# Down projections of a two-layer trunk: 20 of 22 tiles in seven block products, two in plain passes between them, and second weight sums requested from the third product on

## The chip, the cores and the metric

The kernel runs on one core of a Trainium2 chip. The metric is the device time of one execution in microseconds (us). The engines' names are those of the profile: PE is TensorE (matmuls), PEld its weight loads, DVE VectorE, ACT ScalarE, POOL GpSimd, SP the engine that issues most transfers.

## The reference

Two layers; each is a half-step SwiGLU, a gated mixing of three attention branches, and another half-step SwiGLU, with an RMS norm before and after each part. There are 512 tokens of width 1024, the hidden width is 22 x 128 = 2816, and all data is fp32.

```python
def _swiglu(t, w_gate, w_up, w_down):
    return (jax.nn.silu(t @ w_gate) * (t @ w_up)) @ w_down
...
    for l in range(DEPTH):
        f = _swiglu(_rmsnorm(h, ffn1_pre_g[l]), ffn1_w_gate[l], ffn1_w_up[l], ffn1_w_down[l])
        h = h + 0.5 * _rmsnorm(f, ffn1_post_g[l])
        u = _rmsnorm(h, mix_pre_g[l])
        ...
        k_mem, v_mem = jnp.split(mem_n @ w_mem_kv[l], 2, axis=-1)
        ...
        h = h + _rmsnorm(merged @ w_out[l], mix_post_g[l])
        f = _swiglu(_rmsnorm(h, ffn2_pre_g[l]), ffn2_w_gate[l], ffn2_w_up[l], ffn2_w_down[l])
        h = h + 0.5 * _rmsnorm(f, ffn2_post_g[l])
```

What matters here is the last product of `_swiglu`, hidden (512 x 2816) by w_down (2816 x 1024), which occurs four times: the stages are called a0, c0 (the two SwiGLUs of the first layer) and a1, c1, and the mixing between them b0, b1. Also in play are the norm after it, the residual and the next norm, and the norm of the memory tokens, whose keys and values the mixing needs.

## The kernel before

**Arithmetic.** An fp32 matmul is done as three faster ones (`mm3`, L203 to L205) on a high and a low part of each operand. `split` makes the parts: ScalarE casts the high one (L189), VectorE subtracts it to get the low one (L190). So every block of weights of 256 rows by 512 columns (512 KB, in SBUF 128x1024) costs a transfer, a cast `wh_..` and a subtraction `wl_..`; four buffers of each (the tags wh and wl) and four landing tiles (raw) turn round.

**Block products.** A large matrix product is cut 2 x 2 by 2 x 2 and done in seven block products in place of eight, each of a sum of hidden blocks (`aa_..`, made by `first_factor` from the stored hidden halves `hra`) and a sum of weight blocks. `BlockUnit` is one such block of weights, of two 128-row tiles; its sums of two blocks are kept in `bta` tiles, made by a plain transfer followed by an accumulating one on POOL's queue (SUMS, products 2 and 5), or by VectorE's addition of a block onto a kept sum (products 3 and 6, L354). A product runs over both chunks (`ci`) of 8 k-tiles, and over two of the four tiles of 128 tokens (`e`). SUM gives the pair of PSUM banks in which a product accumulates, `pda_0_e`, `pda_1_e` or `pda_2_e`:

```python
    SUM = (0, 1, 2, 0, 2, 0, 0)
    TO = ((0, 0), (0, 0), (1, 1), (0, 1), (0, 1), (1, 1), (1, 0))
```

TO gives the token half and the column half into which the finished bank goes. Between uses by two outputs, a bank's content is copied or added into the result tile `fa_t` (t is the tile of 128 tokens), by ScalarE or by VectorE (L975); the next product then accumulates on top of what the bank holds.

**The down projection.** 16 of the 22 k-tiles go in seven products, in the order 0, 2, 3, 4, 5, 1, 6, and the other six plainly in `down` afterwards, one token tile's half after the other; banks are seeded there from `fa`, and `dst.result` takes the square (ScalarE) and the scaled result (VectorE).

**The order of the work.** A queue of jobs (class `Queue`) writes the program. A job's weights are loaded (cast and subtraction written out) before it starts, and so are those of the four next blocks (`load_ahead`, AHEAD = 4). When landing tiles come free, `fetch_ahead` issues transfers in the order of the jobs. A token tile's norm chain (`Sub.chain`: residual, square, norm, turning by four transposes per bank, split) is woven between matmuls, each step a given modelled time after the one before. Each engine then runs its instructions in the order written.

**Around the change.** The memory norm and the memory keys and values (`mem_norm`, `mem_kv`) come at the end of the first SwiGLU of each layer.

## Time and profile before

| | us |
|---|---|
| median of 3 runs (2341.53 to 2341.89) | 2341.72 |
| the profiled execution | 2341.6 |
| its span, first to last instruction | 2339.8 |
| TensorE busy (99%) | 2326.2 |
| VectorE busy (78%) | 1815.4 |
| ScalarE busy (61%) | 1429.4 |
| GpSimd busy (11%) | 246.6 |

The mean granted TensorE clock is 0.999. A timeline row gives start, duration, engine, line, operation, output and inputs, and in brackets how long the engine had been idle and what ended it. Rows of matmuls overlap: their spacing, not their duration, is what one costs. A row of the windows gives the window, its length, the busy time of each engine with the number of instructions, the clock, the DMA share and GB/s. The names in the profile leave the buffer numbers out, so `pda` is any bank of a0's or a1's down projection, `pdc` any of c0's or c1's.

### The profile page before, as it was taken

What the parts mean: (1) busy time and instruction counts of PE and PEld (TensorE: products, weight loads), DVE (VectorE), ACT (ScalarE), POOL (GpSimd) and SP (SyncE); (2) the same over time, 40 slices, a digit from 0 to 9 for tenths busy, and PEclk for the clock granted to TensorE, in tenths of its full rate; (3) what the DMA queues carried; (4) which work ended last, traced back from release to release, by engine and by line L of the source; (5) the groups of instructions that cost most, each with busy time, mean ns of one, the idle gap of its engine ahead of it and who ended that gap; (6) DMA issues with size and microseconds to landing.
All of it is one profiled execution on the core that took longest, in us unless ns stands there. A gap on an engine that the chain in (4) does not pass through costs nothing.

```text
span 2339.8 us, 32552 instructions
## 1 busy us (share of the span) xinstructions
PE 2326.2 (99%) x12232; PEld 1994.8 (85%) x12232; DVE 1815.4 (78%) x2407; ACT 1429.4 (61%) x2307; POOL 246.6 (11%) x330
## 2 busy tenths in 40 slices
PE   9999999999999999999999999999999999999998
PEld 8888889998888888888888888889988888888887
DVE  8766978676898887769887679786768988866696
ACT  6655766665665465567665567656656655556574
POOL 1101100100122011101011110011001210111110
PEclk9999999999999999999999999999999999999999
DMA  8866858753232676669586767587423326776682
GB/s 247 236 174 181 228 179 249 199 163 108 73 110 72 234 218 182 167 167 256 171 217 170 185 190 228 190 238 227 135 76 91 100 83 232 219 189 169 180 224 99
DMA packets 241697, 412.74 MB, mean 176 GB/s; under 512 B 12650, under 2 KB 78466, under 8 KB 241028
## 3 DMA queue, kind: packets, MB, share of 16 engines
q1 hardware_dynamic: 200992, 326.74, 42.5%
q0 software_dynamic: 37088, 71.34, 17.7%
q10 hardware_dynamic: 3460, 12.59, 1.4%
q8 instruction: 96, 1.57, 0.3%
q14 instruction: 61, 0.50, 0.1%
HBM read 383.35 MB, written 27.26 MB: 175 GB/s over the span
## 4 chain that ended last, share of the span: by engine, by line
PE 90%; DVE 5%; DMA 3%; ACT 1%; issue 1%; SPq 0%; POOL 0%; DVEq 0%; ACTq 0%; POOLq 0%
PE ptc L203 5%; PE ptc L205 5%; PE ptc L204 5%; PE pta L203 5%; PE pta L205 5%; PE pta L204 5%; PE g L203 3%; PE g L204 3%; PE g L205 3%; PE pdc L203 3%; PE pda L205 3%; PE pdc L205 3%; PE pdc L204 3%; PE pda L204 3%; PE pda L203 3%; PE pv L203 1%
## 5 line engine op out<-in xcount | busy, mean ns | idle before, releaser
L190 DVE TENSOR_TENSOR wl_tc<-ktc,wh_tc 128x1024 fp32r<-128x1024 f32 x80 | 97.7, 1223 | 63.3 <-ACT wh_tc L189 63.3
L190 DVE TENSOR_TENSOR wl_ta<-kta,wh_ta 128x1024 fp32r<-128x1024 f32 x80 | 97.6, 1223 | 57.8 <-ACT wh_ta L189 57.8
L205 PE MATMUL pta<-wh_ta,aga 128*128 128x512 f32 x320 | 124.7, 390 | 1.3 <-DVE aga L190 1.3
L189 ACT CAST wh_tc<-ktc 128x1024 fp32r<-128x1024 f32 x80 | 84.1, 1054 | 67.9 <-PE ptc L205 48.0
L203 PE MATMUL pta<-wh_ta,aga 128*128 128x512 f32 x320 | 125.2, 392 | 0.0
L203 PE MATMUL ptc<-wh_tc,agc 128*128 128x512 f32 x320 | 125.1, 393 | 0.0
L205 PE MATMUL ptc<-wh_tc,agc 128*128 128x512 f32 x320 | 124.6, 389 | 0.0
L204 PE MATMUL ptc<-wl_tc,agc 128*128 128x512 f32 x320 | 124.6, 389 | 0.0
L204 PE MATMUL pta<-wl_ta,aga 128*128 128x512 f32 x320 | 124.6, 389 | 0.0
L189 ACT CAST wh_ta<-kta 128x1024 fp32r<-128x1024 f32 x80 | 84.1, 1053 | 65.7 <-PE pta L205 41.8
L190 DVE TENSOR_TENSOR wl_tc<-raw_tc,wh_tc 128x1024 fp32r<-128x1024 f32 x56 | 68.6, 1224 | 45.4 <-ACT wh_tc L189 45.3
L190 DVE TENSOR_TENSOR wl_ta<-raw_ta,wh_ta 128x1024 fp32r<-128x1024 f32 x58 | 70.9, 1224 | 41.9 <-ACT wh_ta L189 41.8
L189 ACT CAST wh_ta<-raw_ta 128x1024 fp32r<-128x1024 f32 x58 | 60.9, 1052 | 45.5 <-PE pta L205 38.0
L189 ACT CAST wh_tc<-raw_tc 128x1024 fp32r<-128x1024 f32 x56 | 59.0, 1054 | 47.8 <-PE ptc L205 36.6
L203 PE MATMUL ptc<-wh_tc,us_b 128*128 128x512 f32 x224 | 87.7, 391 | 0.2
L203 PE MATMUL pda<-wh_da,aa 128*128 128x512 f32 x224 | 87.5, 391 | 0.0
L203 PE MATMUL pdc<-wh_dc,ac 128*128 128x512 f32 x224 | 87.5, 391 | 0.0
L205 PE MATMUL ptc<-wh_tc,us_b 128*128 128x512 f32 x224 | 87.2, 389 | 0.0
L204 PE MATMUL ptc<-wl_tc,us_b 128*128 128x512 f32 x224 | 87.2, 389 | 0.0
L205 PE MATMUL pda<-wh_da,aa 128*128 128x512 f32 x224 | 87.2, 389 | 0.0
L204 PE MATMUL pda<-wl_da,aa 128*128 128x512 f32 x224 | 87.2, 389 | 0.0
L204 PE MATMUL pdc<-wl_dc,ac 128*128 128x512 f32 x224 | 87.2, 389 | 0.0
(593 smaller groups left out, 7932.7 us busy)
## 6 DMA issues: line engine op xcount, KB each, us to landing
raw_ta<-in_ffn_w_gate_dram SPq DMA_DIRECT2D x44, 512.0 KB, 4.4
raw_tc<-in_ffn_w_gate_dram SPq DMA_DIRECT2D x44, 512.0 KB, 4.7
raw_da<-in_ffn_w_down_dram SPq DMA_DIRECT2D x42, 512.0 KB, 3.8
raw_dc<-in_ffn_w_down_dram SPq DMA_DIRECT2D x42, 512.0 KB, 3.6
kta<-in_ffn_w_up_dram SPq DMA_DIRECT2D x40, 512.0 KB, 6.2
raw_wg<-in_w_gate_dram SPq DMA_DIRECT2D x40, 512.0 KB, 4.7
ktc<-in_ffn_w_up_dram SPq DMA_DIRECT2D x40, 512.0 KB, 5.7
kt<-in_w_gate_dram SPq DMA_DIRECT2D x24, 512.0 KB, 5.9
```

The lines of the kernel that those rows point to most:

```text
L189: both = [nc.scalar.copy(h_ap, src)]
L190: make = lambda: nc.vector.tensor_tensor(l_ap, src, h_ap.bitcast(F32), ALU.subtract)
L203: nc.tensor.matmul(pt, lh, rh, start=start, stop=False, skip_group_check=free)
L204: nc.tensor.matmul(pt, lh, rl, start=False, stop=False, skip_group_check=free)
L205: nc.tensor.matmul(pt, ll, rh, start=False, stop=stop, skip_group_check=free)
```

## The change

Twenty of the 22 tiles go in seven products, in three chunks of 8, 8 and 4 k-tiles (ROWS = 4, 4, 2 rows of the 2 x 2 cut). Products 0, 2 and 1 are done for all chunks, then 3 and 4 interleaved, then 5 and 6 for all chunks. The two remaining tiles go in three plain passes, behind the products (2, 1), (1, 0) and (6, 0), written (product, chunk). Product 6's weights get block (1,0) by an accumulating transfer (`adds`) in place of VectorE's addition. The sums for product 5 are requested when the jobs (2, 0), (1, 0) and (3, 0) begin. Tokens 0 and 1 are finished when product 4 ends, tokens 2 and 3, one after the other, in the last chunk of product 6. `down` stays for the mixing's output alone. The memory tokens are normed and turned in a0's third group of gate products and saved to DRAM; they are loaded again at the job (6, 2), and their keys and values are made inside the mixing, behind its first three gate products. The steps of the norm chains are spaced by tables (W_A, W_C).

The largest of the moves, on TensorE, in a0. Before, where product 5 ends (banks `pda_0_..`) and the next product begins:

```order
L203 MATMUL pda_0_1_2101<-wh_da_1_5_2_2395,aa_0_5_2399 128x512
L204 MATMUL pda_0_1_2101<-wl_da_1_5_2_2396,aa_0_5_2399 128x512
L205 MATMUL pda_0_1_2101<-wh_da_1_5_2_2395,aa_0_5_2399 128x512
L203 MATMUL pda_1_0_2432<-wh_da_0_1_0_2436,aa_0_1_2482 128x512 [waits Activation_49]
L204 MATMUL pda_1_0_2432<-wl_da_0_1_0_2437,aa_0_1_2482 128x512 [waits DVE_49]
```

Now, at the same place; `wh_da_2_5_0` is the weight block of chunk 2, product 5, row 0:

```order
L203 MATMUL pda_0_1_2165<-wh_da_2_5_0_2781,aa_2_5_2849 128x512
L204 MATMUL pda_0_1_2165<-wl_da_2_5_0_2782,aa_2_5_2849 128x512
L205 MATMUL pda_0_1_2165<-wh_da_2_5_0_2781,aa_2_5_2849 128x512
L203 MATMUL pda_0_0_2164<-wh_da_0_6_0_2785,aa_0_6_2897 128x512 [waits DVE_49,Activation_49]
L204 MATMUL pda_0_0_2164<-wl_da_0_6_0_2786,aa_0_6_2897 128x512
```

Behind product 5 came product 1 in the banks `pda_1_..`; now comes product 6, in the banks that product 5 has just used. The wait on VectorE in its first row is for the addition of that bank into `fa_2`.

On VectorE, before, around that addition (L975):

```order
L354 TENSOR_TENSOR bta_1_0_1944<-bta_1_0_1944,raw_da_1_1_2_2318 128x1024 [waits DMAHW6_49]
L190 TENSOR_TENSOR wl_da_1_1_0_2475<-raw_da_1_1_0_2312,wh_da_1_1_0_2474 128x1024 [waits DVE_49,Activation_49]
L975 TENSOR_TENSOR fa_2_2094<-fa_2_2094,pda_0_0_2100 128x512 [waits PE_49]
L190 TENSOR_TENSOR wl_da_1_1_2_2479<-raw_da_1_1_2_2318,wh_da_1_1_2_2478 128x1024 [waits Activation_49]
L975 TENSOR_TENSOR fa_3_2095<-fa_3_2095,pda_0_1_2101 128x512 [waits PE_49]
```

Now (L1020), from the residual of token tile 1 on:

```order
L676 SCALAR_TENSOR_TENSOR ha_1_2753<-fa_1_2157,nfa_1_2744,ha_1_2753 128x1024 [waits DMAHW7_49,DVE_49]
L190 TENSOR_TENSOR wl_da_p_2844<-raw_da_p_2495,wh_da_p_2843 128x1024 [waits DMAHW6_49,Activation_49]
L581 TENSOR_SCALAR nha_0_2747<-nha_0_2747 128x1 [waits Activation_49]
L190 TENSOR_TENSOR wl_da_1_6_0_2890<-bta_1_0_2041,wh_da_1_6_0_2889 128x1024 [waits DMASW4_49,Activation_49]
L587 SCALAR_TENSOR_TENSOR nha_0_2747<-nha_0_2747 128x1 [waits DVE_49]
L581 TENSOR_SCALAR nha_1_2748<-nha_1_2748 128x1 [waits Activation_49]
L1020 TENSOR_TENSOR fa_2_2158<-fa_2_2158,pda_0_0_2164 128x512
L588 SCALAR_TENSOR_TENSOR nha_0_2747<-nha_0_2747 128x1 [waits DVE_49]
L587 SCALAR_TENSOR_TENSOR nha_1_2748<-nha_1_2748 128x1 [waits DVE_49,Activation_49]
L683 SCALAR_TENSOR_TENSOR fa_0_2156<-ha_0_2751,nha_0_2747,gqa_2799 128x1024 [waits DMAHW6_49,DVE_49]
L588 SCALAR_TENSOR_TENSOR nha_1_2748<-nha_1_2748 128x1 [waits DVE_49]
L1020 TENSOR_TENSOR fa_3_2159<-fa_3_2159,pda_0_1_2165 128x512 [waits PE_49]
```

The additions stood among the low parts of product 1's weights; now they stand behind the low part of the plain pass's block (`wl_da_p`), that of product 6's second chunk (`wl_da_1_6_0`), and the norm steps of tiles 0 and 1.

On TensorE at the very end (c1), the second half of tile 3 had a bank of its own (`pdc_0_3_1`; the first half's was `pdc_0_3_0`) and none of its rows had a wait. Now both halves are in the bank `pdc_0_1`; where the one ends and the other begins:

```order
L204 MATMUL pdc_0_1_20532<-wl_dc_2_6_0_21272,ac_2_6_21316 128x256
L205 MATMUL pdc_0_1_20532<-wh_dc_2_6_0_21271,ac_2_6_21316 128x256
L203 MATMUL pdc_0_1_20532<-wh_dc_2_6_0_21271,ac_2_6_21316 128x256 [waits DVE_49]
L204 MATMUL pdc_0_1_20532<-wl_dc_2_6_0_21272,ac_2_6_21316 128x256
L205 MATMUL pdc_0_1_20532<-wh_dc_2_6_0_21271,ac_2_6_21316 128x256
```

The row with the wait is the first of the second half; it is for the scaled result of the first half (L656).

The diff, cut to its core:

```diff
-        BLOCKS = {0: (0, 0), 3: (1, 1), 1: (1, 0), 6: (1, 0)}
+        BLOCKS = {0: (0, 0), 3: (1, 1), 4: (1, 1), 1: (1, 0), 6: (1, 0)}
         SUMS = {2: (0, (0, 1), (0, 0)), 5: (1, (1, 1), (0, 1))}
...
-            return self.n in self.BLOCKS and self.twin is None
+            return self.n in self.BLOCKS and self.twin is None and not self.adds
...
+            if self.adds:
+                self.block(self.keep.get(0, self.k0), self.BLOCKS[self.n], accum_op=ALU.add)
...
-                nc.vector.tensor_tensor(src, src, self.raw[:], ALU.add)
+                if not self.adds:
+                    nc.vector.tensor_tensor(src, src, self.raw[:], ALU.add)
...
+    def block_units(order, keep, rows, nm, src, before, pair=None, c0=0, at=0, adding=()):
         made = {}
         for n in order:
             for k in range(0, rows, 2):
                 behind, twin = None, None
+                if n in adding:
+                    behind = made[2 if n == 3 else 3, k]
                 if n in (2, 5):
-                    behind = made[n // 2 * 2 - 2 + n // 5, k] if before is None else before[4 if n == 2 else 5, k]
+                    behind = made[n // 2 * 2 - 2 + n // 5, k] if before is None else before(n, k)
                 if n == 4 or n == 6 and order.index(1) == 5:
                     twin = made[n - 1 if n == 4 else 1, k]
-                made[n, k] = BlockUnit(n, src, rows, k, 2, S, keep, f"{nm}_{n}_{k}", pair, behind, twin)
-                made[n, k].c0 = c0
-        return made, [(n, [made[n, k] for k in range(0, rows, 2)]) for n in order]
+                made[n, k] = un = BlockUnit(n, src, rows, k, min(2, rows), S, keep, f"{nm}_{n}_{k}", pair, behind, twin, n in adding)
+                un.c0, un.at = c0, at + k
+        return made, {n: [made[n, k] for k in range(0, rows, 2)] for n in order}
+    def following(made):
+        return None if made is None else lambda n, k: made[4 if n == 2 else 5, k]
...
+        def __init__(self, name, g_post, g_pre, half, tag, waits=None, sign=(1.0, 1.0)):
+            self.waits, self.sign, self.after = waits or [(W_H, u + n) for u, n in zip(W_U, W_N)], sign, 0
...
-                yield ("wait", W_U[t] + self.slack + (W_N[t] if self.slack == 0.0 else 0.0))
+                yield ("wait", self.waits[t][1])
+                Q.until(self.after)
...
+    W_A = ((4.8, 14.0), (4.8, 14.5), (5.5, 11.0), (7.5, 11.0))
+    W_C = ((4.8, 14.0), (4.8, 14.5), (4.8, 8.5), (6.0, 9.0))
...
+    LAST = (0, 2, 1, 3, 4, 5, 6)
...
+        def factor_parts(ci, n):
+            nm, k = f"a{name}_{ci}_{n}", ROWS[ci]
+            if n == 6 or ci == 2:
+                t = stile([P, 2, k, S // 2], ("k", "tri", "rs")[ci], nm)
+                return t[:, 0], t[:, 1]
+            if ci == 0:
+                st["a", n] = stile([P, 2, 2, k, S // 2], "u", nm)
+            return st["a", n][:, ci, 0], st["a", n][:, ci, 1]
         def first_factor(ci, n):
-            nm = f"{name}_{ci}_{n}"
-            if ci == 0:
-                st["a", n] = stile([P, NC, 2, FC // 2, S // 2], "u", f"a{nm}")
-            h, l = (st["a", n][:, ci, x] for x in range(2))
+            h, l = st["a", n, ci] = factor_parts(ci, n)
...
+        def reload(tiles):
+            if tiles[0] == 0:
+                hT.clear()
+            for t in tiles:
+                hT.append(stile([P, D], "o", f"h{name}_{t}", F32))
+                nc.sync.dma_start(hT[t][:], hsave[t] if src.name != "x" else x[0, t * P:(t + 1) * P, :])
...
+            if (n, ci) == (4, 2):
+                dst.gains(parts=("gp",))
+                reload((0, 1))
+            elif (n, ci) == (5, 0):
+                dst.gains(parts=("gq",))
+                reload((2, 3))
+            elif (n, ci) == (2, 1):
+                st["b", 1] = seeds("mm", f"pd{name}_1", [dst.fs[e][:, HF[0]] for e in range(2)])
...
+            i, hf = TO[n]
+            tiles = [(un, k) for un in uns for k in range(un.nk)]
+            at_end = n == 6 and ci == 2
+            def step(un, k, e, c=FULL):
+                cols, last = slice(e * P, (e + 1) * P), ends and (un, k) == tiles[-1]
+                kk = un.at + k
+                mm3(pts[e][:, c], h[:, kk, cols], l[:, kk, cols], un.h[:, k, c], un.l[:, k, c], opens and (un, k) == tiles[0],
+                    last, free=True)
+                return 3 * (c.stop - c.start) * PE_US
+            if not at_end:
+                steps = [(*one, e) for one, e in itertools.product(tiles, range(2))]
+                if (n, ci) in ((5, 2), (6, 0)):
+                    steps.sort(key=lambda x: x[2])
+                for one in steps:
+                    yield step(*one)
+            else:
+                Q.hold = True
+                for e in range(2):
+                    t = 2 * i + e
+                    parts = HALVES if e and dst.g_pre is None else (FULL,)
+                    for x, c in enumerate(parts):
+                        for un, k in tiles:
+                            yield step(un, k, e, c)
+                        if len(parts) > 1:
+                            dst.last_part(t, hf, c, pts[e][:, c], x)
+                    if len(parts) == 1:
+                        dst.result(t, hf, pts[e][:])
+                        Q.spawn(dst.chain(t))
+                Q.hold = False
                 return
-            i, hf = TO[n]
+            if ci != LATEST[n]:
+                return
             for e in range(2):
                 f = dst.fs[2 * i + e][:, HF[hf]]
                 if n in (4, 5):
                     nc.vector.tensor_tensor(f, f, pts[e][:], ALU.add)
                 else:
                     nc.scalar.copy(f, pts[e][:])
-            if n == 4:
-                st["b", 1] = seeds("z", f"pd{name}_1", [dst.fs[e][:, HF[0]] for e in range(2)])
-        DOWN = [(n, ci) for n in ORDER for ci in range(NC)]
+            for e in range(2):
+                t = 2 * i + e
+                for hf in {4: (1, 0), 5: (1,)}.get(n, ()):
+                    dst.result(t, hf, dst.fs[t][:, HF[hf]])
+                if n == 4:
+                    Q.spawn(dst.chain(t))
+        def plain_down(hf, tokens, un):
+            if 1 in tokens and hf == 1:
+                st["b", 3] = seeds("mm", f"pd{name}_3", [dst.fs[2 + e][:, HF[1]] for e in range(2)])
+            banks = {i: st["b", {(0, 0): 1, (0, 1): 2, (1, 1): 3, (1, 0): 0}[i, hf]] for i in tokens}
+            for i, k, e in itertools.product(tokens, range(un.nk), range(2)):
+                t, cols = st["hid", EARLY + k], slice((2 * i + e) * P, (2 * i + e + 1) * P)
+                mm3(banks[i][e][:], t[:, 0, cols], t[:, 1, cols], un.h[:, k], un.l[:, k], False,
+                    i == 1 and hf == 1 and k == un.nk - 1, free=True)
+                yield 3 * S * PE_US
+                if i == 1 and hf == 1 and k == un.nk - 1:
+                    nc.scalar.copy(dst.fs[2 + e][:, HF[1]], banks[i][e][:])
+        ROWS = (4, 4, 2)
+        DOWN = [(n, ci) for n in LAST[:3] for ci in range(3)]
+        DOWN += [(3, 0), (4, 0), (3, 2), (3, 1), (4, 1), (4, 2)]
+        DOWN += [(n, ci) for n in LAST[5:] for ci in range(3)]
+        LATEST = dict(DOWN)
...
+            def sums(ci, i):
+                if ("bt", ci, i) not in st:
+                    st["bt", ci, i] = stile([P, ROWS[ci], S], ("k", "tri", "v")[ci], f"bt{name}_{ci}_{i}", F32)
+                return st["bt", ci, i]
+            last = st["units"]
+            behind = following(last), following(last), lambda n, k: last[6, 2]
+            rounds = []
+            for ci, rows in enumerate(ROWS):
+                where = lambda i, k0, ci=ci: sums(ci, i)[:, k0:k0 + 2]
+                rounds.append(block_units(LAST, Keep(where), rows, f"d{name}_{ci}", wd[l, ci * FC * P:(ci * FC + 2 * rows) * P],
+                                          behind[ci], adding=(6,))[1])
+            plains = {(2, 1): (0, (0,)), (1, 0): (1, (1, 0)), (6, 0): (0, (1,))}
+            def begin(n, ci):
+                sooner = {(2, 0): 0, (1, 0): 1, (3, 0): 2}.get((n, ci))
+                for un in rounds[sooner][5] if sooner is not None else ():
+                    un.fetch()
+                yield from product(ci, n, rounds[ci][n])
             for n, ci in DOWN:
-                yield rounds[ci][n], (lambda n=n, ci=ci: product(ci, n, rounds[ci][n]))
+                yield rounds[ci][n], (lambda n=n, ci=ci: begin(n, ci)), (n, ci)
+                if (n, ci) in plains:
+                    hf, tokens = plains[n, ci]
+                    un = Unit(wd[l], EARLY, NF - EARLY, hf * S, S, f"d{name}_p{n}", -1.0 if hf else None)
+                    yield [un], (lambda hf=hf, tokens=tokens, un=un: plain_down(hf, tokens, un)), None
...
+            if g == TG[2]:
+                some(2)
+                for _ in range(5):
+                    besides(1)
+                    some(1)
...
-        some(12)
...
+        for uns, run, at in todo:
+            if at == (4, 2):
+                marks["late"] = len(Q.jobs)
+            elif at == (6, 0):
+                dst.after = len(Q.jobs)
+            elif at == (6, 2) and final is not None:
+                Q.add([], lambda: iter(final() or ()))
+            marks["end"] = Q.add(uns, run)
...
+            for x, part in enumerate((h, l)):
+                nc.sync.dma_start(mn_saved[x][:, 2 * i:2 * i + 2], part.rearrange("p (j m) -> p j m", j=2))
...
         Q.add(*todo[1].pop(0))
+        mem_kv(l, mn, ks, vs)
...
+        subs.append(Sub(f"a{l}", (1, l), (2, l), True, "v", W_A, (1.0, -1.0)))
         subs.append(Sub(f"b{l}", (3, l), (4, l), False, "v"))
-        subs.append(Sub(f"c{l}", (5, l), (0, l + 1) if l < L - 1 else None, True, "k"))
+        subs.append(Sub(f"c{l}", (5, l), (0, l + 1) if l < L - 1 else None, True, "v", W_C, (1.0, -1.0)))
...
+        ma = ffn(l, subs[i], ffn1_w_gate, ffn1_w_up, ffn1_w_down, subs[i + 1], f"a{l}", None if l else "v",
+                 () if l else mem_ahead(), lambda l=l, mn=mn: mem_load(l, mn))
+        mb = mixing(l, subs[i + 1], mn, *kvs[l], subs[i + 2])
```

221 lines of the change are left out of this document (74 added, 147 removed).

## The prediction

> **What bounds the kernel now.** I read the page first (busy times, chain), then TensorE's waits, then the windows and the timeline of the first down projection (a0, 237 to 345 us), then the end of the span.
>
> ```profile
> span 2339.8 us, 32552 instructions
> PE 2326.2 (99%) x12232; PEld 1994.8 (85%) x12232; DVE 1815.4 (78%) x2407; ACT 1429.4 (61%) x2307; POOL 246.6 (11%) x330
> PE 90%; DVE 5%; DMA 3%; ACT 1%; issue 1%; SPq 0%; POOL 0%; DVEq 0%; ACTq 0%; POOLq 0%
> ...
> PE pwo L204 <- DVE wl_wo L190: 1.6, 2, 0.9
> PE zf L1367 <- POOL qk L1348: 1.4, 2, 1.0
> PE pta L205 <- DVE aga L190: 1.3, 1, 1.3
> PE warm L1848 <- DVE warm L1932: 1.3, 1, 1.3
> ```
>
> TensorE is busy for 2326.2 of 2339.8 us, and its waits are 1 us here and there; none of them names a tile of a down projection. So the time is the number of matmuls times their spacing, plus what little TensorE stands still. A matmul that is taken out is worth its whole spacing, and a wait that is put in costs its whole length. The spacing, in the first down projection:
>
> ```profile
> 280.66 0.39 PE L203 MATMUL pda<-wh_da,aa 128*128 128x512 f32 x1
> ...
> 290.18 0.39 PE L203 MATMUL pda<-wh_da,aa 128*128 128x512 f32 x1
> ...
> 293.35 0.39 PE L205 MATMUL pda<-wh_da,aa 128*128 128x512 f32 x1
> ```
>
> From the first to the last row are 56 steps (12.69 us): 0.2267 us for a 512-column matmul, without a gap. What feeds it is less easy there:
>
> ```profile
> 240.00:252.00 12.00, 12.00 (x59) 10.03 (x58) 12.00 (x15) 9.96 (x15) 0.80 (x1) 1.00 1.07 321
> 252.00:264.00 12.00, 12.00 (x55) 9.94 (x54) 12.00 (x16) 8.21 (x11) 4.05 (x4) 1.00 1.06 195
> 264.00:276.00 12.00, 12.00 (x55) 9.94 (x54) 12.00 (x18) 8.96 (x13) 0.00 (x0) 1.00 0.59 175
> 276.00:288.00 12.00, 12.00 (x55) 9.94 (x54) 12.00 (x14) 8.78 (x13) 0.00 (x0) 1.00 0.61 222
> 288.00:300.00 12.00, 12.00 (x55) 9.94 (x54) 12.00 (x16) 7.36 (x10) 0.00 (x0) 1.00 0.54 175
> ```
>
> The columns are the window, its length, and busy time of TensorE, its weight load, VectorE, ScalarE and GpSimd, then clock, DMA share and GB/s. VectorE is full for these 60 us and the DMA engines for the first 24, yet TensorE never stops.
>
> **What is taken out.** A down projection had 480 matmuls of 512 columns and has 468 (20 tiles in products are 5 groups of 4 rows' worth, 7 x 60 = 420, and two plain tiles are 48). 12 x 4 x 0.2267 = **-10.9 us**. All other matmuls and transposes stay in number. The additions of block (1,0) for product 6 on VectorE (L354, four of 1.13 us per projection) become accumulating transfers; as TensorE waits for nothing of VectorE's there today, that gives 0.
>
> **The new wait, the main term.** Products 5 and 6 use the same two PSUM banks (SUM gives 0 for both). Before, product 1 stood between them and used others; now (6,0) follows (5,2). Its first matmul must wait until VectorE has added bank pda_0_0 into fa_2 (L1020), and in VectorE's order that addition stands behind wl_da_1_6_0 and nha_1 (front's second excerpt). wl_da_1_6_0 needs its cast on ScalarE, and that cast reuses a weight buffer (four in turn) that the last matmul of (5,2) reads. So from the end of (5,2) on, a chain has to run with TensorE idle. Its pieces have rows in the present trace:
>
> ```profile
> 290.42 1.06 ACT L189 CAST wh_da<-raw_da 128x1024 fp32r<-128x1024 f32 x1 [1.67 <-PE pda L205]
> 298.54 1.06 ACT L189 CAST wh_da<-bta 128x1024 fp32r<-128x1024 f32 x1 [1.35 <-PE pda L205]
> 356.99 1.06 ACT L623 ACTIVATE fa<-ha 128x1024 f32<-128x1024 f32 x1 [0.42 <-DVE ha L665]
> 357.96 0.18 ACT L623 ACTIVATION_READ_ACCUMULATOR fa<-ha 128x1 f32 x1
> ...
> 284.58 1.23 DVE L354 TENSOR_TENSOR bta<-bta,raw_da 128x1024 f32<-128x1024 f32 x1
> 285.71 1.29 DVE L190 TENSOR_TENSOR aa<-hra,aa 128x512 fp32r<-128x512 f32 x2
> 286.92 1.23 DVE L190 TENSOR_TENSOR wl_da<-raw_da,wh_da 128x1024 fp32r<-128x1024 f32 x1
> 293.80 0.69 DVE L975 TENSOR_TENSOR fa<-fa,pda 128x512 f32<-128x512 f32 x1
> 299.67 1.22 DVE L190 TENSOR_TENSOR wl_da<-bta,wh_da 128x1024 fp32r<-128x1024 f32 x1
> 355.02 0.15 DVE L572 TENSOR_SCALAR nha<-nha 128x1 f32<-128x1 f32 x1
> 355.68 1.27 DVE L665 SCALAR_TENSOR_TENSOR ha<-fa,nfa,ha 128x1024 f32<-128x1024 f32 x1
> ```
>
> The cast at 290.42 was let go by a matmul 0.4 us before (the rows are 0.23 apart; one starts 290.18). The low part starts 0.07 us after the cast's end (299.60 to 299.67). So: 0.4 to the cast, 1.06 cast, then two strands side by side, 0.07 + 1.22 low part on VectorE, or 1.06 + 0.18 square of ha_1 on ScalarE with a gap of some 0.1; then 0.15 and a hand-over of 0.1 for L581, 0.69 the addition, 0.1 back to TensorE: 0.4 + 1.06 + 1.3 + 0.25 + 0.69 + 0.1 = 3.8 after the last matmul's start, where the next would come at 0.23: 3.6 idle.
>
> A second strand leads to the same place. VectorE's rows from the addition into fa_1 (allowed when product 4 ends, so when product 5 starts) to that into fa_2 are six of 1024 columns (1.13 apart, 284.58 to 285.71), ten of 512 (0.6 apart), two of L665's kind (1.2) and nine small ones (0.13): 6.8 + 6.0 + 2.4 + 1.2 = 16.4 us. Product 5 is 60 matmuls, 13.6 us. That leaves TensorE 2.8 idle at least, and 3.1 with the hand-overs; the two strands meet, so some of both adds up. Bounds: 3.0 (the second strand alone) and 4.6 (the first, and VectorE 1 us late as well); a gain is excluded, as nothing waits there now. I take **3.7 us**, close above the first strand. In c1 no square of h follows (no next norm): 0.4 + 1.06 + 1.29 + 0.69 + 0.1 - 0.23 = 3.3. Sum 3 x 3.7 + 3.3 = **+14.4 us** (12.0 to 18.4). The addition into fa_3 stands five rows on, 2.2 us of work (three small ones, 1.2, 0.6), while the 12 matmuls on pda_0_0 take 2.7: 0 for that one.
>
> **The end of the span.** Tile 2 and tile 3 now end one after the other, and tile 3's two halves share a bank, where they had one each.
>
> ```profile
> 2333.07 0.28 PE L205 MATMUL pdc<-wh_dc,hidc 128*128 128x256 f32 x1
> 2333.39 0.38 ACT L623 ACTIVATE fe<-pdc 128x256 f32<-128x256 f32 x1 [1.68 <-PE pdc L205]
> 2333.67 0.19 ACT L623 ACTIVATION_READ_ACCUMULATOR fe<-pdc 128x1 f32 x1
> 2333.90 0.42 DVE L645 SCALAR_TENSOR_TENSOR fc<-pdc,gpc 128x256 f32<-128x256 f32 x1 [0.46 <-ACT fe L623]
> 2335.01 1.54 DVE L653 SCALAR_TENSOR_TENSOR hc<-fc,nfc,hc 128x512 f32<-128x512 f32 x3
> ```
>
> The span ends 5.9 us after the product of the second half starts (2333.90 to 2339.8). Counted from the first of tile 3's twelve 256-column matmuls (0.12 apart) that product could start at 11 x 0.12 + 0.83 = 2.15. But the second half's matmuls wait for the first half's product: last matmul 0.6, square at 0.92, its sum at 1.47, product behind tile 2's 512-column one (0.6 to 0.7) until 2.2. So they start at 2.3, and the second product could start at 2.3 + 0.6 + 0.83 = 3.7; on VectorE tile 2's residual (two of 0.68 after small rows) ends at about 4.05. 4.05 - 2.15 = **+1.9 us** (1.0 to 2.5).
>
> **Other places.** From c0 to a1 tile 3's turned tokens now stand directly ahead of the gate matmuls that use them, where twelve matmuls stood between; the copy and the low part of one bank are
>
> ```profile
> 351.12 1.07 ACT L192 ACTIVATE us_a<-uta 128x512 fp32r<-128x512 f32 x2
> 353.62 0.68 DVE L193 SCALAR_TENSOR_TENSOR us_a<-uta,us_a 128x512 fp32r<-128x512 f32 x1
> ```
>
> 0.53 + 0.68 and a hand-over, 1.3 at most, the other bank's matmuls covering a part: **+0.4** (0 to 1.3). From a to b, tokens 2 and 3 are worked out behind three gate products (3 x 24 x 0.2267 = 16.3 us) and the memory keys and values. One tile's chain is, by the durations above, two squares (1.24 each), residual and norm (1.2 each), small ones, the turning and its copy (0.53 + 0.68): 7 to 8 us, two tiles some 15. So it is hidden: 0; were the memory work still ahead of the boundary, the cover would be down to some 1 us. The memory norm's turns move into a0's third group, one per product, each with one ScalarE and one VectorE pass that other products hide: 0.
>
> **Sum**, against the profiled execution's own 2341.6 us (span 2339.8; the median of the runs is 2341.72): 2341.6 - 10.9 + 14.4 + 1.9 + 0.4 = **2347.4**, with 0.1 for the median **2347.5 us**, +0.25%. Its own range by the bounds is 2343.7 to 2353.
>
> **Rivals.**
>
> *The clock falls in the waits.* TensorE has not stood still for 3 us inside this span, only behind it:
>
> ```profile
> 2335.00:2336.00 1.00, 0.00 (x0) 0.00 (x0) 0.99 (x2) 0.00 (x0) 0.00 (x0) 1.00 0.00 0
> 2336.00:2337.00 1.00, 0.00 (x0) 0.00 (x0) 0.55 (x2) 0.00 (x0) 0.00 (x0) 0.62 0.37 141
> 2337.00:2338.00 1.00, 0.00 (x0) 0.00 (x0) 0.00 (x0) 0.00 (x0) 0.00 (x0) 0.50 0.98 348
> ```
>
> The granted clock goes from 1.00 to 0.50 within 2336 to 2337, by 0.62 at 2336.24, which is 2.9 us after the last record's end (2333.35). A wait of 3.7 is longer. How long the clock stays low no row shows; taken as the same 2.9 us, at half speed, each wait loses 1.45 more, four 5.8: 2353.3. Against it: it is one event, at the end of all work. The Trainium skill (TensorE: Matmul & The Clock Gate, What's actually happening) says that the gate watches a free-running window of about 3.4 us, halves the clock after an idle one and needs a busy one to return. By that page's figure, an estimate, one wait in eleven holds a whole window (0.3 of 3.4) and costs up to 1.7 us, so 0.6 us over four waits and a sum of 2348.1. The trace's 2.9 us is shorter than the page's window, so here the page doesn't rule the dearer case out.
>
> *Transfers come late.*
>
> ```profile
> q1 hardware_dynamic: 200992, 326.74, 42.5%
> q0 software_dynamic: 37088, 71.34, 17.7%
> bta<-in_ffn_w_down_dram SPq DMA_DIRECT2D x16, 512.0 KB, 9.2
> bta<-in_ffn_w_down_dram POOLq DMA_DIRECT2D x16, 512.0 KB, 8.1
> ```
>
> A plain block of 0.524 MB costs 0.425 x 2339.8 / 623 = 1.6 us of all engines, an accumulating one 0.177 x 2339.8 / 136 = 3.05. A down projection had 29 plain and 8 accumulating (71 us) and has 28 and 15 (90 us), in some 107 us. On SP the first sums go behind one more plain block than before, into the 24 us where the engines are full (1.07, 1.06). If they miss their products by 2 us in each projection, +8: 2355.5. Against it: sums are wanted in turn, 8 to 9 us to land, and from 264 on 0.4 of the engines is free.
>
> *Waits elsewhere go.* The mixing stage is reordered (memory keys ahead of the queries); the waits quoted above, less the opening one (warm), are 1.6 + 1.4 + 1.3 = 4.3 us. If all went: 2347.5 - 4.3 = 2343.2, no change. For it speaks that later stages start from other moments; against it that the instructions named there keep their order among themselves.
>
> *The other side: the addition is out in time.* If ScalarE and VectorE run ahead through product 5, as they have 10.9 us for it today (two rounds of product 1), TensorE goes from (5,2) into (6,0) without a gap and the first term stands: 2341.6 - 10.9 + 1.9 + 0.4 = 2333.0. It decides as soon as the waits are under some 1 us each. For it speaks that (5,2) does all of pda_0_0 first, 1.36 us before its end; against it the buffer turn, which no running ahead can pass.
>
> **How the numbers follow.** Forecast 0.47 (of it 0.12 below 2346.4), clock 0.12, transfers 0.11, waits elsewhere 0.15, in time 0.15. A measurement of this kernel tells about 0.2% (4.7 us) from no change, so 2337.0 to 2346.4 counts as the same. Slower 0.35 + 0.12 + 0.11 = 0.58; same 0.12 + 0.15 = 0.27; faster 0.15. The range, 2334 to 2355, reaches from nearly the case in time to most of the two dear ones.
>
> **What would show it.** In the changed trace TensorE's waits should name pda L203 behind VectorE's L1020, four times, 3.0 to 4.6 us each, at the start of product 6, with the cast of wh_da_1_6_0 starting only after (5,2). Another wait of 1.6 us stands before pdc's last six matmuls. The spacing stays 0.2267. A clock under 1.00 in those windows is the first rival; waits on btX low parts behind POOL's transfers the second. If product 6 starts within 1 us of (5,2), the main term is wrong.

## The result, and the profile after

The changed kernel took 2409.79 us (median of 4 runs, 2408.85 to 2410.37); runs of the kernel before beside them took 2341.53 to 2342.4. The ratio is 1.029 (95% interval 1.0272 to 1.0307): 68 us slower. The forecast was slower, by 6 us. The profiled execution took 2410.2 us.

The page of the changed kernel, its span, busy times, shares of the chain of work that ended last, queues and the sums' transfers:

```profile
span 2408.4 us, 32575 instructions
PE 2339.4 (97%) x12172; PEld 1993.4 (83%) x12172; DVE 1817.0 (75%) x2427; ACT 1425.2 (59%) x2314; POOL 280.3 (12%) x358
PE 72%; DVE 11%; DMA 10%; issue 4%; ACT 2%; POOL 0%; SPq 0%; DVEq 0%; ACTq 0%; POOLq 0%
...
q1 hardware_dynamic: 201056, 326.74, 41.2%
q0 software_dynamic: 44704, 86.02, 20.4%
...
bta<-in_ffn_w_down_dram POOLq DMA_DIRECT2D x30, 512.0 KB, 11.5
```

TensorE was 90% of the chain before and is 72%; of the 18 points VectorE has taken 6 and the DMA engines 7. Sixty fewer matmul records, yet TensorE is busy longer, which fits a slower clock. TensorE's waits, changed kernel:

```profile
PE pda L203 <- DVE nha L588: 15.0, 2, 7.5
PE pda L204 <- DVE wl_da L190: 12.8, 8, 2.7
PE pdc L204 <- DVE wl_dc L190: 11.4, 9, 3.2
PE pdc L203 <- DVE nhc L588: 7.5, 1, 7.5
PE pdc L203 <- DVE fc L1020: 4.0, 1, 4.0
...
PE pdc L203 <- DVE fc L656: 1.2, 1, 1.2
```

Before, no row named a tile of a down projection. Rows 1, 4 and 5 are the passage from product 5 to product 6 in the four projections. (VectorE's small norm steps, nha L588, come out last by the profile's clock; they follow the addition L1020 directly.) Rows 2 and 3 are new: low parts of weights that come late within the products.

The windows of a0, in the columns explained in the prediction:

```profile
264.00:276.00 12.00, 12.00 (x54) 9.89 (x54) 12.00 (x16) 11.24 (x17) 2.43 (x2) 1.00 0.79 228
276.00:288.00 12.00, 10.66 (x48) 8.50 (x47) 6.30 (x8) 3.27 (x4) 0.00 (x0) 1.00 0.75 185
288.00:300.00 12.00, 9.60 (x36) 7.43 (x35) 10.22 (x11) 7.57 (x11) 3.69 (x3) 0.86 0.80 216
300.00:312.00 12.00, 11.89 (x53) 9.47 (x52) 7.71 (x10) 4.73 (x5) 3.67 (x3) 1.00 1.09 267
312.00:324.00 12.00, 12.00 (x55) 9.93 (x54) 11.62 (x14) 8.80 (x13) 2.43 (x2) 1.00 1.09 290
324.00:336.00 12.00, 10.57 (x47) 8.43 (x45) 5.73 (x9) 6.57 (x14) 0.00 (x0) 1.00 0.86 258
336.00:348.00 12.00, 3.67 (x13) 2.50 (x14) 12.00 (x24) 7.86 (x18) 0.00 (x0) 0.76 0.34 121
348.00:360.00 12.00, 12.00 (x51) 9.71 (x50) 8.07 (x11) 4.85 (x8) 0.00 (x0) 0.82 0.23 79
```

Two places lose time: the end of product 1 and the start of product 3 (276 to 300; product 3 starts at 291.3), where VectorE is idle for half a window, and the end of product 5 (324 to 348), where VectorE is first idle for 6 us and then full while TensorE stands. After each the clock is under 1.00.

**The second place.** VectorE (all rows but the last) and TensorE (the last row), changed kernel, a0:

```profile
332.81 2.50 DVE L639 SCALAR_TENSOR_TENSOR fa<-fa,gpa 128x512 f32<-128x512 f32 x4 [6.27 <-DMA gpa<-in_ffn_post_g_dram]
...
344.07 1.22 DVE L190 TENSOR_TENSOR wl_da_p<-raw_da_p,wh_da_p 128x1024 fp32r<-128x1024 f32 x1
...
345.27 1.21 DVE L190 TENSOR_TENSOR wl_da<-bta,wh_da 128x1024 fp32r<-128x1024 f32 x1
...
346.60 0.67 DVE L1020 TENSOR_TENSOR fa<-fa,pda 128x512 f32<-128x512 f32 x1
...
347.42 0.77 PE L203 MATMUL pda<-wh_da,aa 128*128 128x512 f32 x1 [7.49 <-DVE nha L588]
```

VectorE waits 6.27 us for the post-norm's gain row `gpa`, needed by the first step of finishing tokens 0 and 1 (L639). From 332.81 on it works without a gap to the addition at 346.60. The gain row, changed kernel and then kernel before (from its issue):

```profile
L137 SPq DMA_DIRECT2D gpa<-in_ffn_post_g_dram x2: 340/340/340, 316.2 to 1513.4; - x2
...
DMA to landing us min/median/max: 16.6/16.6/16.6
```

```profile
L137 SPq DMA_DIRECT2D gpa<-in_ffn_post_g_dram x2: 328/330/332, 279.5 to 1440.2; - x2
...
DMA to landing us min/median/max: 6.3/6.3/6.3
```

It is requested at 316 where the engines are at 1.09, and takes 16.6 us. It is not alone: the 512 KB blocks of the next weights (`raw_wg`) requested beside it, at 313.7 and 317.3, take 13.8 and 16.7 us. In c1 it is there in time and VectorE has no gap; there the wait is 4.1 us.

**The first place.** VectorE's waits for blocks of product 3, changed kernel (the kernel before has no such rows):

```profile
DVE btc L358 <- DMA raw_dc<-in_ffn_w_down_dram: 25.6, 8, 5.8
DVE bta L358 <- DMA raw_da<-in_ffn_w_down_dram: 24.8, 8, 6.3
DVE fa L639 <- DMA gpa<-in_ffn_post_g_dram: 12.3, 2, 6.3
DVE fc L639 <- DMA gpc<-in_ffn_post_g_dram: 5.6, 1, 5.6
```

and the rows of VectorE, POOL and TensorE there:

```profile
271.34 2.56 POOL L329 DMA_DIRECT2D bta<-in_ffn_w_down_dram  x2 [17.90 <-DMA bta<-in_ffn_w_down_dram]
283.58 1.23 DVE L358 TENSOR_TENSOR bta<-bta,raw_da 128x1024 f32<-128x1024 f32 x1 [5.70 <-DMA raw_da<-in_ffn_w_down_dram]
291.71 1.23 DVE L358 TENSOR_TENSOR bta<-bta,raw_da 128x1024 f32<-128x1024 f32 x1 [1.10 <-DMA raw_da<-in_ffn_w_down_dram]
291.34 0.39 PE L203 MATMUL pda<-wh_da,aa 128*128 128x512 f32 x1
294.13 0.61 PE L204 MATMUL pda<-wl_da,aa 128*128 128x512 f32 x1 [2.40 <-DVE wl_da L190]
294.54 0.63 PE L205 MATMUL pda<-wh_da,aa 128*128 128x512 f32 x1
294.97 0.63 PE L203 MATMUL pda<-wh_da,aa 128*128 128x512 f32 x1
295.39 0.63 PE L204 MATMUL pda<-wl_da,aa 128*128 128x512 f32 x1
```

At 271 POOL issues two accumulating transfers for product 5, some 50 us before that product starts (323.3). The plain blocks issued behind them, at 274.4 and 277.3, take 9.2 and 8.7 us to land; in run 3 below, without the early sums, such blocks take 3.4 to 4.7. VectorE adds product 3's blocks ahead of the low parts of product 1's last rows, so TensorE waits there first (at 286.0) and again in product 3 (at 294.1). Behind the second wait the matmuls are 0.427 us apart, not 0.2267: half speed.

**The sum.** TensorE's spacings beyond 0.2267 us, where they are longer by 0.25 us or more (those near 0.427 counted apart, as slow clock), us:

| | a0 | c0 | a1 | c1 | sum |
|---|---|---|---|---|---|
| waits | 15.6 | 15.8 | 16.5 | 11.9 | 59.8 |
| of them 5 to 6 | 7.66 | 7.66 | 7.69 | 4.12 | 27.1 |
| slow clock | 3.7 | 3.9 | 4.3 | 3.1 | 15.1 |

Beside the 27.1 the waits are some 23.3 in products up to 4 (17.8 of them at the two places just named, behind product 3's blocks), 7.1 at the last blocks of product 5 (a0, c0, a1, where L639 holds VectorE up), 1.3 between the halves at the end, and 1 in small ones. 59.8 + 15.1 - 10.9 (fewer matmuls) = 64 of 68; the rest, about 4, is 1.5 outside the down projections and, within them, many steps longer by less than 0.25 us. All steps that end at a matmul of a down projection sum to 501.3 us, 434.3 before the change; all other steps to 1899.0, 1897.6 before.

### The profile page after: what moved, and what is told of

It reads as the page before. It is cut to its first block, busy times and chain, and to the rows that moved or that the text cites. A ratio compares the mean times of both kernels' runs of the same rounds, so it can differ in the third digit from the quotient of the medians.

```text
span 2408.4 us, 32575 instructions
## 1 busy us (share of the span) xinstructions
PE 2339.4 (97%) x12172; PEld 1993.4 (83%) x12172; DVE 1817.0 (75%) x2427; ACT 1425.2 (59%) x2314; POOL 280.3 (12%) x358
## 4 chain that ended last, share of the span: by engine, by line
PE 72%; DVE 11%; DMA 10%; issue 4%; ACT 2%; POOL 0%; SPq 0%; DVEq 0%; ACTq 0%; POOLq 0%
PE ptc L203 5%; PE ptc L204 5%; PE ptc L205 5%; PE pta L203 5%; PE pta L205 5%; PE pta L204 5%; PE g L203 3%; PE g L204 3%; PE g L205 3%; DMA raw_dc<-in_ffn_w_down_dram 2%; DMA raw_da<-in_ffn_w_down_dram 2%; DVE wl_dc L190 2%; DMA bta<-in_ffn_w_down_dram 2%; DVE wl_da L190 1%; DMA gpa<-in_ffn_post_g_dram 1%
## 5 line engine op out<-in xcount | busy, mean ns | idle before, releaser
L203 PE MATMUL pda<-wh_da,aa 128*128 128x512 f32 x280 | 113.3, 405 | 15.0 <-DVE nha L588 15.0
L204 PE MATMUL pda<-wl_da,aa 128*128 128x512 f32 x280 | 113.8, 406 | 12.8 <-DVE wl_da L190 12.8
L203 PE MATMUL pdc<-wh_dc,ac 128*128 128x512 f32 (+1 forms) x282 | 113.4, 402 | 12.7 <-DVE nhc L588 7.5
L204 PE MATMUL pdc<-wl_dc,ac 128*128 128x512 f32 (+1 forms) x282 | 113.2, 402 | 11.4 <-DVE wl_dc L190 11.4
L205 PE MATMUL pda<-wh_da,aa 128*128 128x512 f32 x280 | 112.8, 403 | 0.9 <-DVE aa L190 0.7
L205 PE MATMUL pdc<-wh_dc,ac 128*128 128x512 f32 (+1 forms) x282 | 112.9, 400 | 0.6 <-DVE ac L190 0.3
L190 DVE TENSOR_TENSOR wl_wg<-kt,wh_wg 128x1024 fp32r<-128x1024 f32 x48 | 58.7, 1224 | 43.8 <-ACT wh_wg L189 43.7
```

Source lines behind the costliest of these rows:

```text
L190: make = lambda: nc.vector.tensor_tensor(l_ap, src, h_ap.bitcast(F32), ALU.subtract)
L203: nc.tensor.matmul(pt, lh, rh, start=start, stop=False, skip_group_check=free)
L204: nc.tensor.matmul(pt, lh, rl, start=False, stop=False, skip_group_check=free)
L205: nc.tensor.matmul(pt, ll, rh, start=False, stop=stop, skip_group_check=free)
```

## The experiments

The theory after the result: two causes, the early transfers for product 5 (product 3's waits, the gain row's landing) and VectorE's order (the addition behind the finishing of tokens 0 and 1). Each experiment starts from the changed kernel. Product 5 to 6 stands for the wait between them. Times are medians of 2 to 6 executions; the kernel before beside them took 2340.95 to 2341.86.

| run | us | ratio to before (95%) | 5 to 6 in a0, c0, a1, c1 |
|---|---|---|---|
| changed kernel | 2409.79 | 1.0272 to 1.0307 | 7.66, 7.66, 7.69, 4.12 |
| 1 no gain row | 2390.14 | 1.0180 to 1.0239 | 4.16, 3.46, 4.15, 4.17 |
| 2 addition first | 2402.27 | 1.0231 to 1.0291 | 6.35, 5.39, 6.36, 3.02 |
| 3 no early sums | 2411.99 | 1.0273 to 1.0333 | 6.21, 7.67, 6.31, 7.68 |
| 4 product 6 by VectorE | 2415.08 | 1.0286 to 1.0346 | 8.23, 8.19, 8.19, 8.22 |
| 5 product 5 by VectorE | 2375.30 | 1.0116 to 1.0175 | 4.73, 4.73, 4.76, 4.75 |
| 6 addition first, finishing later | 2374.52 | 1.0113 to 1.0172 | 0.53 |
| 7 both 5 and 6 | 2354.92 | 1.0042 to 1.0087 | 0.53 |
| 8 transfers later | 2354.86 | 1.0035 to 1.0069 | 0.54 |
| 9 turn later | 2354.23 | 1.0039 to 1.0069 | 0.54 |
| 10 sum on GpSimd | 2385.77 | 1.0174 to 1.0206 | 0.54 |
| 11 an eighth of the sum | 2350.13 | 1.0023 to 1.0048 | 0.54 |

**1, without the wait for the gain row.** L639 of the results written in `product` reads its own source in place of the gain row, so these results are multiplied by themselves and not by the gain.

```diff
-            nc.vector.scalar_tensor_tensor(dst, src, c, self.gp[:, HF[hf]], ALU.mult, ALU.mult)
+            nc.vector.scalar_tensor_tensor(dst, src, c, src if own else self.gp[:, HF[hf]], ALU.mult, ALU.mult)
```

> The scaled results of tokens 0 to 3 that read a finished bank's copy (L639) are multiplied by themselves in place of the gain row, so they no longer wait for its transfer, which is still made; the output norm's gain is left out there. Theory (the gain row lands late and holds VectorE's queue): the wait between products 5 and 6 falls from 7.7 us to c1's 4.1 in a0, c0 and a1, the 2.0 to 2.7 us at the last block of product 5 go, and some slow clock with them: 17 to 20 us less, about 2391 us. Rival (VectorE's own work is the bound there, the gain row only stands beside it): within 4 us of 2410.

2390.14 us, 19.7 less. Its TensorE row at the start of product 6, and its waits:

```profile
341.82 0.77 PE L203 MATMUL pda<-wh_da,aa 128*128 128x512 f32 x1 [4.00 <-DVE nha L588]
```

```profile
PE pdc L204 <- DVE wl_dc L190: 10.0, 7, 2.9
PE pda L204 <- DVE wl_da L190: 9.5, 7, 2.4
PE pda L203 <- DVE nha L588: 8.0, 2, 4.0
```

The wait falls to 3.5 to 4.2 in all four, 15.9 in all, and those at the end of product 5 are gone; product 3's stay. So the gain row cost 11 us between the products, 7 before that and a part of the slow clock, and what is left is close to the forecast's 14.4.

**2, the addition first.** The loading of product 6's next block is held back and written behind the two additions.

```diff
+            if (n, ci) == (5, 1):
+                Q.hold = True
...
+            if n == 5:
+                Q.load_ahead()
```

> The load of block (6,1), row 0, is written out behind the two additions of product 5's banks, not ahead of them; nothing else moves. If the order (the cast that waits for the last matmul of product 5, then its low part, then the addition) makes the wait, as predicted: 2 to 3 us less in each projection, the most in c1 (4.1 to about 1.5), 2400 to 2404 us. If VectorE is late anyway because of the gain row: 1 to 1.5 us less each in a0, c0, a1, about 2404 us. If the order is without effect: 2410.

2402.27 us: the wait falls by 1.1 to 2.3 us in each. The time lies in the range of the first case, but not for its reason: the most was expected in c1 (to about 1.5), which gave the least and keeps 3.0. The buffer turn with its cast and low part is one to two us of the wait; the rest is the finishing of tokens 0 and 1 ahead of the addition, in a0, c0 and a1 with its wait for the gain row.

**3, product 5's sums not requested early.**

```diff
-                sooner = {(2, 0): 0, (1, 0): 1, (3, 0): 2}.get((n, ci))
+                sooner = None
```

> The weight sums of product 5 are requested in the order of the jobs, not when products 2, 1 and 3 begin. Theory (the early accumulating transfers stand in the way of product 3's blocks): the waits in products 2 to 4, 23 us over four projections, and the slow clock behind them fall by more than half, 12 to 20 us less, unless product 5 then waits for its sums: 2392 to 2400 us. Rival (the landing tiles come free too late for those blocks, whoever uses the transfer engines): within 4 us of 2410 or slower.

2411.99 us, no gain. Product 3's waits are gone, so these requests made them. But product 5 now waits for its own sums, in its TensorE waits:

```profile
PE pda L203 <- ACT wh_da L189: 5.8, 2, 3.4
PE pdc L203 <- ACT wh_dc L189: 5.4, 2, 2.8
```

The same transfers collide with the later stretch instead, where the gain row now takes 22.1 us to land.

**4, product 6's second block as before**, by a plain transfer and VectorE's addition.

```diff
-                                          behind[ci], adding=(6,))[1])
+                                          behind[ci])[1])
```

> Product 6's block (1,0) comes by a plain transfer and VectorE's addition (L358), as before the change: five accumulating transfers less per projection (some 3.0 us of all engines each), five plain ones more (1.6 us), five additions of 1.13 us more on VectorE. Theory (the load on the transfer engines makes the waits before product 5 and the late gain row): 7 us of transfer time less per projection, 10 to 20 us faster, about 2395 us. Rival (VectorE is the bound from product 4 on): the wait between 5 and 6 grows by 2 to 4 us each, 2418 us.

2415.08 us, 5 slower, near the rival's 2418. Product 3's waits stay (1.4 and 2.4 in a0): product 6's accumulating transfers do not cause them. But the gain row now lands in 6.2 us (a0 and a1) and VectorE's wait for it is gone: these transfers are a part of what made it late. The wait is 8.2 all the same, in all four, c1 too: in a0 VectorE, with five more additions ahead of L1020, works without a gap from 322 to the addition at 347. So these additions are not free in the new order, although in the kernel before nothing waited for them.

**5, product 5's second block by VectorE**, from the landing tile of products 3 and 4, which hold the same block (1,1); its first block stays a plain transfer. This takes five accumulating transfers out of each projection.

```diff
-                tc.keep_in_program_order(self.block(t, one))
-                tc.keep_in_program_order(self.block(t, two, accum_op=ALU.add))
+                if self.plus:
+                    self.block(t, two)
...
+            if self.n == 4 and self.plus is not None:
+                self.plus.fetch()
+                both = self.plus.keep.get(1, self.plus.k0)
+                nc.vector.tensor_tensor(both, both, self.raw[:], ALU.add)
```

> Product 5's sum is made by a plain transfer of block (0,1), requested as in the change, and VectorE's addition of block (1,1), which lies in the landing tile of products 3 and 4: five accumulating transfers less per projection without a plain one more (15 us of all engines), five additions of 1.13 us more on VectorE. Theory (the transfer engines are overloaded and the order is bad besides): the 23 us of waits in products 2 to 4 and most of the slow clock behind them go, the gain row lands in time, the wait between 5 and 6 falls to c1's 4.1: 2410 - 23 - 11 - 7 - 8, about 2362 us (2352 to 2375). Rival (order and VectorE's work alone): the additions lengthen VectorE's row, 2405 or more.

2375.30 us, 34.5 less, at the upper end of the theory's range; the wait between 5 and 6 falls to 4.7, not 4.1. From its page, its gain row's answer, and VectorE's waits:

```profile
q0 software_dynamic: 39264, 75.54, 18.4%
```

```profile
DMA to landing us min/median/max: 8.2/8.3/8.4
```

```profile
DVE bta L362 <- DMA raw_da<-in_ffn_w_down_dram: 4.1, 2, 2.2
DVE btc L362 <- DMA raw_dc<-in_ffn_w_down_dram: 3.8, 2, 1.9
```

10.5 MB less on the software queue, and three things go together: VectorE's waits for product 3's blocks fall from 50.4 us to 7.9, the gain row lands in 8.3 instead of 16.6, and its wait vanishes from VectorE's list. The gain row is thus late for the transfers' sake: either set of five taken out, product 5's here or product 6's in run 4, brings it down to 6 to 8 us.

**6, the addition first and the finishing later**: experiment 2, and results, residual and norm of tokens 0 and 1 start a modelled 13 us after product 4 (with the later steps drawn together).

```diff
-    W_A = ((4.8, 14.0), (4.8, 14.5), (5.5, 11.0), (7.5, 11.0))
+    W_A = ((4.8, 4.0), (4.8, 4.5), (5.5, 11.0), (7.5, 11.0))
...
-                    Q.spawn(dst.chain(t))
+                    Q.spawn(finished(t), 13.0)
+        def finished(t):
+            for hf in (1, 0):
+                dst.result(t, hf, dst.fs[t][:, HF[hf]])
+            yield from dst.chain(t)
```

> The load of block (6,1) behind the two additions, and the scaled results, residuals and norms of tokens 0 and 1 written out some 13 us later, in product 6; the transfers are as in the change. Theory (from product 4's end to the addition VectorE has 16.4 us of work against product 5's 13.6, and the gain row holds it): without the 5 us of results and residuals and without the gain row there, the wait between 5 and 6 is under 1.5 us in all four, the one at the last block of product 5 is gone; the waits in products 2 to 4 stay. 27 + 7 - 4 + some slow clock less: 2372 to 2382 us. Rival (only the transfers count): the waits stay above 4 us, 2400 or more.

2374.52 us, 35.3 less, as expected, with the gain row as slow as ever (16.1 us to land) and product 3's waits in place:

```profile
PE pdc L204 <- DVE wl_dc L190: 11.2, 7, 3.2
PE pda L204 <- DVE wl_da L190: 8.9, 8, 2.6
```

The passage from 5 to 6 costs 0.53. It is a matter of what is written ahead of the addition, on VectorE, and not of the banks or the buffer turn as such. The finishing put off was not run without the other edit.

**7, both.**

> The two edits before together. If transfers and order are separate causes and the only ones: the down projections run without waits but for the start of the last halves in c1, 12 x 4 x 0.2267 us less than before the change, plus about 2 us at the end: 2331 to 2338 us, faster than the kernel before. If the work put off collides in product 6 or at the boundaries: 2340 to 2350 us.

2354.92 us, 54.9 less, and slower than both forecasts. 34.5 and 35.3 added up would be 69.8: each takes away a part of the passage from 5 to 6. Its rows at that passage, VectorE and TensorE:

```profile
331.51 1.23 DVE L190 TENSOR_TENSOR wl_da_p<-raw_da_p,wh_da_p 128x1024 fp32r<-128x1024 f32 x1 [1.49 <-ACT wh_da_p L189]
332.66 1.28 DVE L1030 TENSOR_TENSOR fa<-fa,pda 128x512 f32<-128x512 f32 x2
...
333.48 0.47 PE L203 MATMUL pda<-wh_da,aa 128*128 128x512 f32 x1 [0.37 <-DVE fa L1030]
```

The addition now waits for the bank alone, and the clock is 0.999 again. Left are 3 to 4 us of waits per projection, 13 to 15 in four. Summed as above, the steps of the down projections come to 438.6 us, 4.3 more than before the change (waits, less the matmuls taken out); all others come to 1906.4, 8.8 more. So two thirds of what keeps this kernel behind stands outside the down projections, for the most part at the turning of the tokens put off and the first matmuls behind it (in a0 and a1 each 1.04 at the turning, 0.65, 0.3 and 0.26 at the gate product).

**8 and 9, the transfers later, then the turn later.** In 8 product 5's plain transfers are requested at (2,1), (1,0), (1,1) and kept in program order; 9 also sets tokens 0 and 1's turning 2 us later.

```diff
-                sooner = {(2, 0): 0, (1, 0): 1, (3, 0): 2}.get((n, ci))
+                sooner = {(2, 1): 0, (1, 0): 1, (1, 1): 2}.get((n, ci))
...
-    W_A = ((4.8, 4.0), (4.8, 4.5), (5.5, 11.0), (7.5, 11.0))
+    W_A = ((4.8, 6.0), (4.8, 6.5), (5.5, 11.0), (7.5, 11.0))
```

> The kernel with both mends (the sum for product 5 added by VectorE, the addition out of the bank and its block's loading first, results of tokens 0 and 1 13 us later; 2354.92 us), and the plain transfers for product 5 moved from the starts of (2,0), (1,0), (3,0) to those of (2,1), (1,0), (1,1) and kept in program order. Theory (the small waits that are left in a0 at 263, 1.0 us, and 303, 1.4 us, come of these early transfers standing ahead of blocks that are wanted first): the wait at 263 goes, and the one at 303 falls to 0.5 or less, in all four projections: 2354.9 - 4 x (1.0 + 0.9) = 2347.3 us (2345 to 2350). Rival (they come of VectorE, which is full from 264 to 292 us, with two more additions of 1.13 us per projection than the kernel before): both waits stay, 2354 to 2356.

> The run before it in this table, and the turning of tokens 0 and 1 set 2 us later in the tables of steps. Theory (the 1.0 us wait at the first transposes, which stand ahead of the norm step that they read, is a matter of spacing): it goes in a0, c0 and a1, 3 us less than the run before it: some 2344 us (2342 to 2347), no difference from the kernel before that can be told. Rival (the norm chain of these tokens is held by ScalarE or VectorE and moves along with the turn): the wait stays, less than 1 us changes.

2354.86 and 2354.23 us: no difference. Both theories missed; the times are those of the rivals. In a0 the wait at 263 fell from 1.0 to 0.5 and 0.4, that at 302 from 1.4 to 1.1 and 1.0; in the others the latter stayed at 1.3 to 1.5, and so did the 1.05 at the turning in a0 and a1. So the last two are not a matter of spacing or of these transfers' dates.

**10 and 11, VectorE's share of what is left**, from 9. In 10 GpSimd does product 5's additions; in 11 VectorE does them on a part of the columns (its rows show 128x128, so an eighth, not the sixteenth that its expectation speaks of).

```diff
-                nc.vector.tensor_tensor(both, both, self.raw[:], ALU.add)
+                nc.gpsimd.tensor_tensor(both, both, self.raw[:], ALU.add)
```

> The run with the later turn (2354.23 us), and the five additions per projection of the sum for product 5 (128x1024, 1.13 us each on VectorE) done by GpSimd, which is busy 11% of its span, in place of VectorE. Theory (the 1.0 to 1.5 us wait in front of the factor sum at 302 us in a0 comes of the additions that stand ahead of it on VectorE): it goes in all four projections, 4 x 1.2 = 4.8 less: 2349 us (2346 to 2351). Rival (GpSimd's additions are so slow, or stand so far behind its transfers, that landing tiles come free late): raw tiles and the sums' low parts are waited for, 2355 to 2375.

> The run with the later turn (2354.23 us), and the same five additions per projection done on 64 of 1024 columns only: 15/16 of the sum's second block is left out, so the output differs; transfers, order and waits stay. It measures what VectorE's time for them costs on the end. Theory (VectorE's time is what is left in products 3 and 4): the waits at 262 and 302 go, 4 x 1.3 to 4 x 1.8 less: 2347 to 2349 us. Rival (they come of transfers): the waits stay, 2353 to 2355.

GpSimd's groups in 10, and TensorE's waits:

```profile
L369 POOL TENSOR_TENSOR bta<-bta,raw_da 128x1024 f32<-128x1024 f32 x10 | 31.1, 3114 | 72.4 <-DMA raw_da<-in_ffn_w_down_dram 65.6 <-DMA bta<-in_ffn_w_down_dram 6.8
```

```profile
PE pdc L204 <- DVE wl_dc L190: 11.7, 6, 4.3
PE pda L204 <- DVE wl_da L190: 9.2, 4, 4.1
```

3.1 us for an addition that costs VectorE 1.13: 2385.77 us, as the rival had it and 11 us beyond its range. In 11 the wait at 302 is gone from a0, a1 and c1 and is 0.4 in c0, and the time is 2350.13, 4.1 less, just above the theory's range: that wait was VectorE's time. The one near 262 (1.0) stays in a0 and c0; its cause is open. Even without these additions the kernel is 0.2 to 0.5% slower than before. No version run here beats the kernel before: what is left is small waits in several places, each a few tenths to 1.5 us, most of them outside the down projections.

## Why the prediction was right or wrong

The forecast was 2347.5 us and the time is 2409.8. Of the 62 us between them, 12.7 are in the main term, 23.3 in the products up to 4, most of it waits for transfers, and 7.1 at the end of product 5, both put at nothing in the sum, and 15.1 in the clock, which was put at nothing too.

**Right: the side, and the matmuls taken out.** The spacing stayed 0.2267 wherever the clock was full, so -10.9 stands. The wait for VectorE's addition came at all four places named. The end behaved as worked out: a wait of 1.3 us between the halves, and 6.8 us from the last matmul to the end of the span, where it was 6.7; +1.4 against +1.9 (1.0 to 2.5). At the boundary from c0 to a1 a wait of 0.8 appeared (forecast 0.4, at most 1.3).

**Wrong: the size of "the new wait, the main term".** 27.1 us for 14.4, outside its bounds of 12.0 to 18.4. The strand itself was counted rightly: c1, where the gain row is in time, shows 4.1 for 3.3, and with the gain row's wait taken away the four come to 15.9. What failed is the step of the 16.4 us for VectorE from one addition to the next: it summed durations and took for granted that VectorE would run through them. Among the ten stand the L639, which read a gain row; the change requests this row later than before (316 instead of 280 in a0), among a crowd of transfers. Its landing was put at nothing, and it stood 6.3 us in the way, with another 7 us at the last blocks of product 5.

**Wrong: that the buffer turn decides.** The argument against the rival of an addition out in time, "the buffer turn, which no running ahead can pass", was true of the order as written alone. Experiment 6 passes it by writing the addition first. Nor does the turn make most of the wait: with the block's load written behind (run 2), c1 keeps 3.0 of its 4.1 us, which are the second strand, VectorE's row of work.

**The rival "transfers come late" was right in kind and more than twice too small.** It priced +8 with first sums for product 2 missed by 2 us. The misses are product 3's plain blocks, behind early accumulating transfers for product 5: 17.8 us of waits, of 23.3 in the products up to 4. The estimate of 90 us of transfers in some 107 was made over the whole projection; what mattered was that the early requests put them into the stretch where product 3 wants its own blocks. The step that failed is the argument against this rival, that "from 264 on 0.4 of the engines is free": that was so in the kernel before, while in the changed one the engines are at 0.75 to 1.09 from 276 to 336, and at 0.34 and 0.23 in the two windows after. Experiments 3 and 5 show it. Run 4 shows that the other new transfers, product 6's, do not delay product 3's blocks but do delay the gain row.

**The rival "the clock falls" was right too, at 15.1 instead of 5.8 us.** It was priced at 1.45 us for each of four waits; there were eight waits of 2.3 us or more, two in each projection, at 1.9 us each.

**"Waits elsewhere go"** did not happen: the waits at pwo, zf, pta and warm are 1.2, 1.7, 1.2 and 1.3 (1.6, 1.4, 1.3 and 1.3 before), and a new one of 1.5 came, at a turning at the program's start (of the eleven runs only 6 and 10 have one of 1 us or more there).

The rivals were treated as alternatives, each with a chance of its own. They came together: one crowd of transfers delays blocks and gain row, the delays make waits long enough for the clock to fall. Added to the sum, 8 and 5.8 would have given 2361.3: 20 of the 68 us.

## What to carry to other kernels

When a chain on one engine is priced by summing durations, list every operand on it that comes by DMA, gain rows included, and find in the windows how busy the DMA engines are when it is requested. A transfer that is requested early is not free because it is wanted late: here it went ahead of those that were wanted now, and an accumulating one weighed nearly twice a plain one (3.0 against 1.6 us of all engines, from the two queues' shares). Where a bank is reused at once, write the instruction that frees it ahead of the other work of its engine; here it was worth 7.5 us ahead of the next block's load alone (run 2), and 35 with the finishing of two token tiles put off as well (run 6).
